# One plain gate pair per layer instead of two in a fp32 decoder trunk, and the block sums of h taken in another order

## The chip, the cores and the metric

The kernel runs on one core of one Trainium2 chip. The metric is the device time in microseconds of one execution, and smaller is better. The core has a matrix engine (TensorE, PE in the profile), a vector engine (VectorE, DVE), a scalar engine (ScalarE, ACT), a general engine (GpSimd, POOL), and queues of DMA transfers that here are issued by SyncE (SP). Each engine has its own list of instructions and takes them in the order of that list; semaphores tie the lists together.

## The reference

Two layers of a decoder trunk over 1024 tokens with 1024 features, all in fp32:

```
h = rmsnorm(x, norm1[l])
proj = h @ w_in[l]                      # q, k, v of two mixers, and gate_pre (2 x 1024 columns)
o_a = dilated_mixture(...)              # 12 heads: near and far windows, ALiBi softmax
o_b = stick_breaking_attention(...)     # 4 heads: sigmoid(z) times a running product of 1 - sigmoid(z)
gates = sigmoid(gate_pre + b_gate[l])
merged = g_a * (o_a @ w_br[l, :256]) + g_b * (o_b @ w_br[l, 256:])
x = x + merged @ w_o[l]
h2 = rmsnorm(x, norm2[l])               # then a gated FFN with a causal conv, and its residual
```

After the layers comes a last rmsnorm. What matters here is the product `h @ w_in[l]`, above all its 2048 gate columns, and the stick-breaking attention that runs beside it.

## The kernel before, in words

**Precision.** Every fp32 operand of a product is split in two: `split` (L136 to L149) casts the high part on ACT (L139) and subtracts it on DVE to get the low part (L146). A product then takes three matmuls per block of 128 rows: high by high, high by low, low by high.

**Plain and seven.** The feature-major h of one layer stands in SBUF as `hh`, `hl` for two token halves n = 0, 1 (tags hh0, hl0, hh1, hl1), each with 8 blocks of 128 features. `gate(l, c)` (L1207) computes one block of 128 gate columns plainly: two halves of 8 blocks by three matmuls, 48 matmuls of 512 columns. `pair(...)` (L1053) computes two such blocks together by Strassen's scheme in the form with seven products (`seven`, L980): seven products of 4 blocks by three matmuls, 84 matmuls of 512 columns where two plain blocks take 96. For that it needs sums of the quarters of the weights (made on POOL at L1075, L1076 and on DVE at L1080, L1085, and split by `piece`) and sums of the quarters of h.

**The sums of h** are made once per layer by `block_sums` (L989). The quarters are b11, b12, b21, b22 (b11 is half 1, first four blocks; b12 half 0, first four; b21 half 1, last four; b22 half 0, last four). The program's S[1] is b12 - b11, S[2] is b22 - S[1], S[3] is b22 - b12, and S[4] is b21 - S[2]. `first(t, a, b, i)` makes block i of S[1] or S[3] on POOL with three additions (L999, L1004, L1005), `second(i)` makes S[2] on DVE from S[1] in place (L1012, L1013), `fourth(i)` makes S[4] on DVE (L1019 to L1021) into the room of a quarter of h that is no longer needed. `in_two(t, i)` splits a block. In the kernel before, POOL makes the four blocks of S[3] and then the four of S[1]; the splits of S[3] come when the head is over, and S[1] and S[2] follow at a set pace.

**The order of a mixer.** `mixer` (L1229) first drives the head (`head`, L593: the values and the first key and query columns, all plain). Then `attend` walks the attention items: 16 stick items, 4 near items, 16 far items. Between the matmuls of the attention it puts steps of the class `Dense`, at a rate for each kind of item (`RATE`, `RATE_N`, `RATE_T`). `Dense.choose` takes the plain gates first, then the pairs of `main`, and when those are through the gate pairs of `seven`. `PLAIN` is the number of plain blocks (two for each gate pair), and `EARLY` how many of the gate pairs stand early in `main` instead of in the last list. `Dense.side` is the list of the work on the sums; one entry is taken at each step for which its condition holds, and what is left when the first pair starts is done at once. The last dense steps, `finish`, run after the attention.

**Who decides the order.** PE's order is the order of the program. The other engines' lists are put in order by the planner of the framework, by priorities and its own estimate of times.

**Rooms that matter.** The tag `s` has two PSUM banks, for the scores z of the attention: a z can only be written when ACT has read the z two before it, as `beta` (L687) and as `stay` (L688). The tag `xa` has four rooms in SBUF: `kv`, `slots`, a `stay` tile for each stick item, and the sum for S[3]. The tag `ql` has two: the values `vb` of the head, the sum for S[1] and S[2], and the weights `in_a` of each pair. The first column block of each score is masked by POOL (L691); DVE then runs the product along each row (the scan at L704) and multiplies (L708); PE turns the result (`sb_t`, L716) and applies it to the values (`sb_o`, L729).

Of the kernel before, what the change touches and what calls it, by code (L numbers as in the profile page):

```python
# [42 lines left out]
SECOND = 0.35  # L43
RATE = (1.1, 1.25, 1.35, 1.4)
RATE_N = 0.75
RATE_T = 0.6
PLAIN = 4
EARLY = 3
LEAD = 6
LEAD_N = 7  # L50
LEAD_T = 3
# [6 lines left out]
def f32(ap):  # L58
    return ap.bitcast(F32)
# [3 lines left out]
def trunk_kernel(ctx, tc, x, norm1, w_in, b_gate, w_br, w_o, norm2, w_up, conv_w, conv_b, w_down, norm_f, out, depth=None, probe=None):  # L63
# [59 lines left out]
    def bank(tag, name):  # L123
        return ps.tile([P, 512], F32, tag=tag, name=name)
# [4 lines left out]
    def big(name, dtype=F32):  # L129
        return sb.tile([P, 2, T], dtype, tag="e8", bufs=6, name=name)  # L130

    def quarter(name, dtype=F32, c=HF):
        return sb.tile([P, 2048 // c, c], dtype, tag="xa", bufs=4, name=name)
# [41 lines left out]
    def product(o, pairs, first=True, last=True, share=False):  # L175

        n = len(pairs)
        quantum = 2 * 512 // o.shape[-1]
        for i, ((lh, ll), (rh, rl)) in enumerate(pairs):
            pe.matmul(o, lh, rh, start=(first and i == 0), stop=False, skip_group_check=share)  # L180
            pe.matmul(o, lh, rl, start=False, stop=False, skip_group_check=share)  # L181
            pe.matmul(o, ll, rh, start=False, stop=(last and i == n - 1), skip_group_check=share)  # L182
            if i % quantum == quantum - 1 and i < n - 1:
                yield
# [249 lines left out]
    def h_part(n, k):  # L434
        return H[n][0][:, k, :], H[n][1][:, k, :]
# [105 lines left out]
    R = {}  # L541

    def new_v(name):
        return [sb.tile([P, 4, 4, P], F32R, tag="ql", bufs=2, name=name) for _ in range(2)]

    def values_part(vt, w, ms):
        for m in ms:
            o = bank("ps", "v_ps")
            for j in range(2):
                t = 2 * m + j  # L550
                n, c = t // 4, t % 4
                tok = slice(c * P, (c + 1) * P)
                pairs = []
                for k in range(KD):
                    hh, hl = h_part(n, k)
                    pairs.append(((hh[:, tok], hl[:, tok]), w[k]))
                yield from product(o[:, j * 256 : (j + 1) * 256], pairs)
                if j == 0:
                    yield
            ov = o.rearrange("p (j h c) -> p h j c", j=2, h=4)  # L560
            vv = vt[m // 2][:, :, 2 * (m % 2) : 2 * (m % 2) + 2, :]
            one = act.copy(vv[:, :, :, 0:64], ov)
            two = dve.tensor_tensor(vv[:, :, :, 64:128], ov, f32(vv[:, :, :, 0:64]), ALU.subtract)
            LAST["head"] = one.ins.name, two.ins.name
            if m % 2:
                nc.sync.dma_start(sv[0][:, :, 2 * m - 2 : 2 * m + 2, :], f32(vt[m // 2]))
            yield
# [25 lines left out]
    def head(l):  # L593


        def place(n, name):
            x = [big(name, F32R) for _ in range(n)]
            return ([x[0][:, h, :] for h in range(2)] if n == 1 else [y.rearrange("p a b -> p (a b)") for y in x])

        wv = weights(w_in[l][:, OFF_VB : OFF_VB + 256], 256, place(2, "v_w")) if l else early.pop("wv")  # L600
        others = lambda: [weights(w_in[l][:, off : off + P], P, place(1, "kq_w"), None if l else pool) for off in (OFF_KB, OFF_QB)]
        if l:
            wk, wq = others()
        yield
        vt = new_v("vb")
        if l:
            yield from values_part(vt, wv, range(2))
        else:
            yield from values_part(vt, wv, range(1))
            wk, wq = others()  # L610
            yield from values_part(vt, wv, range(1, 2))
        for n in range(2):
            yield from kq_half(0, wk, n)
            yield from kq_half(1, wq, n)
            if n == 0 and not l:
                yield from values_part(vt, wv, range(2, 4))
        if l:
            yield from values_part(vt, wv, range(2, 4))

    def scores(o, qt, ql, k):  # L620
# [368 lines left out]
    def block_sums(dense):  # L989


        last, rs = {}, {}

        def first(t, a, b, i):
            if i == 0:
                new_s(t)
                rs[t] = quarter("h_sum") if t == 3 else sb.tile([P, 4, HF], F32, tag="ql", bufs=2, name="h_sum")
            r, (ah, al), (bh, bl) = rs[t][:, i, :], a()[i], b()[i]
            one = pool.tensor_tensor(r, f32(al), f32(bl), ALU.subtract)  # L999
            if last:  # L1000
                tc.add_manual_dep(one.ins, last["sum"], NO_SYNC, reason="one sum after the other")
            else:
                tc.add_manual_dep(one.ins, LAST["h"], SYNC, reason="after h")
            pool.tensor_tensor(r, r, f32(ah), ALU.add)  # L1004
            last["sum"] = pool.tensor_tensor(r, r, f32(bh), ALU.subtract).ins.name  # L1005

        def second(i):
            if i == 0:
                new_s(2)
            in_two(1, i)  # L1010
            r, (ah, al) = rs[1][:, i, :], b22()[i]
            dve.tensor_tensor(r, f32(ah), r, ALU.subtract)  # L1012
            dve.tensor_tensor(r, r, f32(al), ALU.add)  # L1013

        def fourth(i):
            if i == 0:
                S[4] = half(0, 0)
            r, (ah, al) = small("h_sum"), b21()[i]
            dve.tensor_tensor(r, f32(ah), f32(S[2][i][0]), ALU.subtract)  # L1019
            dve.tensor_tensor(r, r, f32(S[2][i][1]), ALU.subtract)  # L1020
            dve.tensor_tensor(r, r, f32(al), ALU.add)  # L1021
            split(*S[4][i], r, "waits")

        def in_two(t, i):
            split(*S[t][i], rs[3 if t == 3 else 1][:, i, :], "waits", LAST["head"])

        b11, b12, b21, b22 = (lambda n=n, k=k: half(n, k) for k in range(2) for n in (1, 0))
        todo = []

        def series(after, lag, gap, f, g):  # L1030

            at = {}
            for i in range(4):
                at.setdefault(i * gap, []).append(lambda i=i: f(i))
                at.setdefault(i * gap + lag, []).append(lambda i=i: g(i))
            for k in range(3 * gap + lag + 1):
                todo.append((after, lambda fs=at.get(k, ()): [h() for h in fs]))

        for i in range(4):
            todo.append((set(), lambda i=i: first(3, b22, b12, i)))  # L1040
        for i in range(4):
            todo.append(({"head"}, lambda i=i: in_two(3, i)))
        series({"head"}, 5, 2, lambda i: first(1, b12, b11, i), second)
        for i in range(4):
            todo.append((set(), lambda i=i: in_two(2, i)))

        def begin():
            for i in range(4):
                dense.at(1 + 2 * i, lambda i=i: fourth(i))

        return todo, begin

    def pair(dense, l, offs, tiled, put):  # L1053

# [174 lines left out]
    def mixer(l, pending):  # L1229
        R.clear()  # L1230
        vectors = setup(l)
        dense = Dense()
        dense.plain = [gate(l, c) for c in range(PLAIN)]
        gates = [pair_gate(dense, l, e) for e in range(PLAIN // 2, KD)]
        dense.seven = gates[EARLY:]
        dense.side, dense.begin = block_sums(dense)
        dense.done |= {"K0", "K1", "V0", "V1", "V2", "V3"}
        if l:
            next(vectors)
# [24 lines left out]
        for _ in vectors:  # L1264
            pass
        dense.main = [
            *((None, set(), f, True) for f in (pair_near(dense, l, 2), *gates[:EARLY], pair_v(dense, l, 0), pair_near(dense, l, 4), pair_near(dense, l, 6))),
            *((None, set(), f, True) for f in (pair_v(dense, l, 1), pair_kq(dense, l, 1, 0), pair_kq(dense, l, 2, 0))),
# [7 lines left out]
        for pr in range(2):  # L1276
            share = {}
            for i in range(8):
                if i % 4 == 0:
                    share = {}  # L1280
                items.append((f"T{pr}{i}", [f"F{8 * pr + i}"], [], RATE_T, lambda pr=pr, i=i, share=share: far_item(dense, pr, i // 4, i % 4, share)))
        dense.fetch()
# [8 lines left out]
        def in_two(nm, halves=range(2)):  # L1291
            src = R["ob" if nm == "b" else "on"]
            if nm not in oh:
                oh[nm] = big("oh_" + nm, F32R), big("ol_" + nm, F32R)
            hi, lo = oh[nm]
            for n in halves:
                for c in range(2):
                    sl = slice(n * HF, (n + 1) * HF)
                    one = split(hi[:, c, sl], lo[:, c, sl], src[:, c, sl])
                    if nm == "b" and n:  # L1300
                        yields(one)

        branches()
        todo = [(n, e0 + i) for e0 in range(0, KD, 2) for n in range(2) for i in range(2)]
# [782 lines left out]
```

## Time and profile before

| | |
|---|---|
| Median of 3 runs | 2643.44 us (2640.93 to 2643.49) |
| The profiled execution, its own time | 2642.11 us |
| Its span, first to last instruction | 2640.1 us |
| Granted TensorE clock, mean | 1.000 |
| Layer 0: end of the head, first plain gate matmul | 65.0 us |
| Layer 0: first matmul of a pair | 120.5 us |
| Layer 1: first plain gate matmul | 1370.9 us |
| Layer 1: first matmul of a pair | 1424.9 us |

How to read the rows: a timeline row has the start in us from the start of the span, the duration in us, the engine, the line, the operation, the tiles written and read, the shape, and in brackets the idle time before it and what ended it. Matmuls overlap in the pipeline, so what one costs is read from the distance between starts and not from its own duration. A row of the waits has who waited for whom, the total in us, the number of times, and the longest.

### The profile page before, as it was taken

How to read it: one execution, taken by the hardware profiler on the slowest of the kernel's cores; microseconds unless marked ns; L12 is line 12 of the kernel's file. 1: busy time of each engine (PE TensorE's matmuls, PEld its weight loads, DVE VectorE, ACT ScalarE, POOL GpSimd, SP SyncE). 2: the span in 40 equal slices, each digit the busy share in tenths (PEclk: the TensorE clock that was granted, in tenths of full speed). 3: DMA queues.
4: the chain of work that ended last, by engine and by line, in shares of the span. 5: the costliest groups of instructions: out<-in, count | busy, mean ns of one | idle time of the engine just before them, and what ended most of it. 6: DMA issues, size and time to landing. Idle time of an engine off the chain costs nothing.

```text
span 2640.1 us, 36792 instructions
## 1 busy us (share of the span) xinstructions
PE 2621.5 (99%) x12780; PEld 2192.0 (83%) x12780; DVE 2068.6 (78%) x3094; ACT 1337.7 (51%) x2488; POOL 734.9 (28%) x612
## 2 busy tenths in 40 slices
PE   9999999999999999999999999999999999999999
PEld 8888888888888888888888888888888888888888
DVE  5887766795888898897659787667858888888865
ACT  5555565564545555432435555666645455554225
POOL 5422201132244343321162212101321343334200
PEclk9999999999999999999999999999999999999999
DMA  7343587873244444688442445797632544357863
GB/s 259 114 144 112 159 220 204 220 253 90 81 146 146 164 146 157 234 310 322 155 154 93 145 140 160 198 236 203 219 101 80 168 144 159 136 176 256 330 247 116
DMA packets 400550, 468.25 MB, mean 177 GB/s; under 512 B 24437, under 2 KB 315629, under 8 KB 398573
## 3 DMA queue, kind: packets, MB, share of 16 engines
q1 hardware_dynamic: 400348, 465.90, 54.9%
q8 instruction: 101, 1.65, 0.3%
q14 instruction: 85, 0.69, 0.1%
q10 hardware_dynamic: 16, 0.00, 0.0%
HBM read 303.23 MB, written 162.59 MB: 176 GB/s over the span
## 4 chain that ended last, share of the span: by engine, by line
PE 83%; DVE 9%; issue 3%; DMA 2%; ACT 2%; POOL 1%; SPq 0%; DVEq 0%; POOLq 0%; ACTq 0%
PE u_a L983 5%; PE u_a L985 5%; PE u_a L984 5%; PE d_ps L1715 5%; PE d_ps L1716 5%; PE d_ps L1717 5%; PE i_a L983 4%; PE i_a L985 4%; PE i_a L984 4%; PE u_c L985 3%; PE u_c L983 3%; PE u_c L984 3%; PE o_ps L180 2%; PE o_ps L181 2%; PE o_ps L182 2%
## 5 line engine op out<-in xcount | busy, mean ns | idle before, releaser
L146 DVE TENSOR_TENSOR w_lo<-up_a,w_hi 128x512 fp32r<-128x512 f32 x240 | 236.7, 992 | 20.2 <-ACT w_hi L139 20.2
L139 ACT CAST w_hi<-up_a 128x512 fp32r<-128x512 f32 x240 | 149.4, 623 | 183.9 <-PE u_a L984 45.9
L1723 DVE TENSOR_TENSOR x<-x,d_ps 128x512 f32<-128x512 f32 (+1 forms) x228 | 151.8, 671 | 78.0 <-PE d_ps L1717 76.6
L1454 POOL TENSOR_TENSOR cv<-cv 128x512 f32<-128x512 f32 x88 | 131.8, 1509 | 248.8 <-DVE cv L1449 138.9
L139 ACT CAST w_hi<-in_a 128x512 fp32r<-128x512 f32 x192 | 119.2, 621 | 117.5 <-PE i_c L984 42.7
L146 DVE TENSOR_TENSOR w_lo<-in_a,w_hi 128x512 fp32r<-128x512 f32 x192 | 141.3, 736 | 36.4 <-ACT w_hi L139 27.0
L146 DVE TENSOR_TENSOR g<-cv,g 128x512 fp32r<-128x512 f32 x154 | 151.7, 986 | 5.2 <-ACT g L139 2.8
L1715 PE MATMUL d_ps<-gd_in,w_hi 128*128 128x512 f32 (+1 forms) x340 | 130.3, 383 | 2.3 <-ACT w_hi L139 1.4
L1717 PE MATMUL d_ps<-gd_in,w_lo 128*128 128x512 f32 (+1 forms) x340 | 129.8, 382 | 0.0
L1716 PE MATMUL d_ps<-gd_in,w_hi 128*128 128x512 f32 (+1 forms) x340 | 129.8, 382 | 0.0
L1075 POOL TENSOR_TENSOR u<-in_a 128x512 f32<-128x512 f32 x32 | 45.8, 1431 | 293.2 <-DMA in_a<-in_w_in_dram 110.5
L983 PE MATMUL u_a<-hh,w_hi 128*128 128x512 f32 x320 | 124.7, 390 | 0.4 <-DVE u L1605 0.3
L984 PE MATMUL u_a<-t_lo,w_hi 128*128 128x512 f32 x320 | 124.5, 389 | 0.0
L985 PE MATMUL u_a<-t_hi,w_lo 128*128 128x512 f32 x320 | 124.5, 389 | 0.0
L985 PE MATMUL u_a<-hh,w_lo 128*128 128x512 f32 x320 | 124.5, 389 | 0.0
L983 PE MATMUL u_a<-t_hi,w_hi 128*128 128x512 f32 x320 | 124.5, 389 | 0.0
L984 PE MATMUL u_a<-hl,w_hi 128*128 128x512 f32 x320 | 124.5, 389 | 0.0
L146 DVE TENSOR_TENSOR w_lo<-w_raw,w_hi 128x512 fp32r<-128x512 f32 x96 | 77.5, 809 | 57.6 <-ACT w_hi L139 52.8
L691 POOL TENSOR_SCALAR_AFFINE_SELECT beta<-beta 128x128 f32<-128x128 f32 x64 | 36.6, 571 | 305.2 <-ACT beta L687 305.2
L139 ACT CAST g<-cv 128x512 fp32r<-128x512 f32 x154 | 94.9, 616 | 39.8 <-POOL cv L1454 29.3
L1715 PE MATMUL d_ps<-gd_in,wd 128*128 128x512 f32 (+1 forms) x292 | 113.9, 390 | 0.0
L1717 PE MATMUL d_ps<-gd_in,wd 128*128 128x512 f32 (+1 forms) x292 | 112.8, 386 | 0.0
(395 smaller groups left out, 8638.0 us busy)
## 6 DMA issues: line engine op xcount, KB each, us to landing
gd<-g SPq DMA_DIRECT2D x154, 512.0 KB, 3.1
gd_in<-gd SPq DMA_DIRECT2D x154, 512.0 KB, 6.3
up_a<-in_w_up_dram SPq DMA_DIRECT2D x80, 512.0 KB, 5.6
in_a<-in_w_in_dram SPq DMA_DIRECT2D x64, 512.0 KB, 5.4
wd_raw<-in_w_down_dram SPq DMA_DIRECT2D x22, 1024.0 KB
gin<-gs SPq DMA_DIRECT2D x32, 512.0 KB, 5.1
w_raw<-in_w_o_dram SPq DMA_DIRECT2D x64, 256.0 KB, 2.9
t_kq<-tk SPq DMA_DIRECT2D x32, 384.0 KB, 5.0
```

The lines of the kernel that those rows point to most:

```text
L139: one = act.copy(hi, src)
L146: two = dve.tensor_tensor(lo, src, f32(hi), ALU.subtract)
L180: pe.matmul(o, lh, rh, start=(first and i == 0), stop=False, skip_group_check=share)
L181: pe.matmul(o, lh, rl, start=False, stop=False, skip_group_check=share)
L983: pe.matmul(o, w[0][:, c], rh, start=(first and i == 0), stop=False, skip_group_check=True)
L984: pe.matmul(o, w[0][:, c], rl, start=False, stop=False, skip_group_check=True)
L985: pe.matmul(o, w[1][:, c], rh, start=False, stop=(last and i == 3), skip_group_check=True)
L1454: return lambda: pool.tensor_tensor(dst, a, b, ALU.subtract)
L1715: pe.matmul(o[:, sub], wh[:, c], gh[:, sub], start=(i == 0 and k in (0, 4, 5)), stop=False, skip_group_check=True)
L1716: pe.matmul(o[:, sub], wh[:, c], gl[:, sub], start=False, stop=False, skip_group_check=True)
L1717: pe.matmul(o[:, sub], wl[:, c], gh[:, sub], start=False, stop=(i == m - 1), skip_group_check=True)
L1723: dve.tensor_tensor(x, x, o[:, sub], ALU.add)
```

## The change

Four constants change, `RATE_T` from 0.6 to 0.55, `PLAIN` from 4 to 2, `EARLY` from 3 to 4. Per layer, one gate pair that was two plain blocks becomes a pair by seven products, and of the seven gate pairs four stand in `main` (three of six before). The order of the work on the sums changes: POOL makes S[1] first, in a new function `mid` that the head calls, together with the splits of S[1]'s first two blocks. The third split, and S[3] on POOL, follow when the head is over (`go`), then S[2] with the last split of S[1] and the splits of S[2] (`later`), and the splits of S[3] last. In layer 0 `mid` is called behind the last values of the head, with the second half of the keys and queries still to come; in layer 1 it is called ahead of the last values.

```
-RATE_T = 0.6
-PLAIN = 4
-EARLY = 3
+RATE_T = 0.55
+PLAIN = 2
+EARLY = 4
 ...
             yield from kq_half(1, wq, n)
             if n == 0 and not l:
                 yield from values_part(vt, wv, range(2, 4))
+                R["mid"]()
         if l:
+            R["mid"]()
             yield from values_part(vt, wv, range(2, 4))
 ...
         def second(i):
             if i == 0:
                 new_s(2)
-            in_two(1, i)
             r, (ah, al) = rs[1][:, i, :], b22()[i]
 ...
-        todo = []
-        def series(after, lag, gap, f, g):
-            at = {}
-            for i in range(4):
-                at.setdefault(i * gap, []).append(lambda i=i: f(i))
-                at.setdefault(i * gap + lag, []).append(lambda i=i: g(i))
-            for k in range(3 * gap + lag + 1):
-                todo.append((after, lambda fs=at.get(k, ()): [h() for h in fs]))
-        for i in range(4):
-            todo.append((set(), lambda i=i: first(3, b22, b12, i)))
-        for i in range(4):
-            todo.append(({"head"}, lambda i=i: in_two(3, i)))
-        series({"head"}, 5, 2, lambda i: first(1, b12, b11, i), second)
-        for i in range(4):
-            todo.append((set(), lambda i=i: in_two(2, i)))
+        def mid():
+            for i in range(4):
+                first(1, b12, b11, i)
+            for i in range(2):
+                in_two(1, i)
+        def go():
+            in_two(1, 2)
+            for i in range(4):
+                first(3, b22, b12, i)
+        def later(i):
+            second(i)
+            if i == 0:
+                in_two(1, 3)
+            else:
+                in_two(2, i - 1)
+        todo = [({"head"}, go)]
+        todo += [(set(), lambda i=i: later(i)) for i in range(4)]
+        todo += [(set(), lambda: in_two(2, 3))]
+        todo += [(set(), lambda i=i: in_two(3, i)) for i in range(4)]
 ...
-        return todo, begin
+        return todo, begin, mid
 ...
-        dense.side, dense.begin = block_sums(dense)
+        dense.side, dense.begin, R["mid"] = block_sums(dense)
```

## The prediction

> **What bounds the kernel now.** I read the totals of the page first, then TensorE's own waits.
>
> ```profile
> PE 2621.5 (99%) x12780; PEld 2192.0 (83%) x12780; DVE 2068.6 (78%) x3094; ACT 1337.7 (51%) x2488; POOL 734.9 (28%) x612
> ```
>
> ```profile
> PE z L621 <- ACT stay L688: 2.7, 5, 1.1
> ...
> PE u_ps L181 <- DVE hl L536: 1.3, 2, 0.7
> ...
> PE o L900 <- DVE p1l L146: 0.4, 2, 0.2
> ```
>
> PE is busy 2621.5 of 2640.1 us, and the longest group of its waits is 2.7 us in all. So a matmul less is time less, and a wait that PE gains is never given back: nothing behind it has slack on PE to take it in. I work against the profiled execution (2642.11 us by its own time, 2 us of it outside the span); the median of the runs shown is 1.3 us above, and the difference that I find is put on the median.
>
> **The gain.** One key product of 24 matmuls of 512 columns runs between these two starts:
>
> ```profile
> 1342.31 0.39 PE L180 MATMUL q_ps<-hh,kq_w 128*128 128x512 f32 x1
> ...
> 1347.75 0.39 PE L180 MATMUL kq_ps<-hh,kq_w 128*128 128x512 f32 x1
> ```
>
> 5.44 us for 24 is 0.227 us each. A plain pair takes 96, a pair by seven 84, so a layer loses 12 and the kernel 24, **-5.4 us** (the built lists of PE differ by just these 24). 0.2% of this kernel, about what a measurement can tell from no change, is 5.3 us, so the gain alone would stand on the edge of it. Transfers for the weights stay at 1 MB a pair. A pair by seven adds to DVE 7 splits, 2 sums and 3 additions, and saves 4 splits; to ACT 7 casts and 4 copies for 4 casts and 4 copies; to POOL 2 sums. With DVE at 78% and PE hardly waiting for it, I put these at nothing where they are spread out; what they cost without cover is a rival below. The lower `RATE_T` and the later place of one gate pair move dense work from the far items into the end of the attention: the same matmuls, between -1 and +1 us, as PE's wait there now is 0.4 us in all (o, L900), taken as 0.
>
> **The first wait: layer 0.** What changes is what stands ahead of the first scores. In the built lists of the changed kernel, ACT has this order in layer 0 (tiles' numbers left out; in brackets whom it waits for):
>
> ```
> t_hi<-h_sum x3  (blocks 0 to 2 of S[3]) [Pool]
> t_hi<-h_sum, gt<-g_ps, t_hi<-h_sum
> w_hi<-in_a      (first weight piece)
> w_hi<-in_a      (the summed piece)      [Pool]
> gt<-g_ps, table load, beta<-z, stay<-z
> ```
>
> The second `w_hi` casts what POOL writes at L1076, and POOL's list has the eight sums, then L1075 and L1076 of the first pair. Both were far from the first scores before, because there 192 plain matmuls stood ahead of the first pair; now it is 96. The first scores need not wait for the pair, but they stand behind it on ACT.
>
> ```profile
> 43.26 1.30 POOL L999 TENSOR_TENSOR h_sum<-hl 128x512 f32<-128x512 f32 x1 [14.11 <-DVE hl L146]
> 44.61 0.95 POOL L648 MEMSET slots<- 64x1024 f32 x1
> 45.64 1.29 POOL L1004 TENSOR_TENSOR h_sum<-h_sum,hh 128x512 f32<-128x512 f32 x1
> ...
> 75.17 1.74 POOL L999 TENSOR_TENSOR h_sum<-hl,hl 128x512 f32<-128x512 f32 x1
> ...
> 78.68 1.27 POOL L1005 TENSOR_TENSOR h_sum<-h_sum,hh 128x512 f32<-128x512 f32 x1
> ...
> 98.46 1.30 POOL L1075 TENSOR_TENSOR u<-in_a 128x512 f32<-128x512 f32 x1 [4.73 <-DVE w_lo L146]
> 99.84 1.63 POOL L1076 TENSOR_TENSOR in_a<-in_a 128x512 f32<-128x512 f32 x1
> ```
>
> ```profile
> 76.03 0.62 ACT L139 CAST w_hi<-w_raw 128x512 fp32r<-128x512 f32 x1 [2.10 <-PE g_ps L181]
> 76.56 0.58 ACT L1216 COPY gt<-g_ps 128x512 f32<-128x512 f32 x1
> 77.15 1.28 ACT L687 ACT_TABLE_LOAD   x1
> 78.45 0.60 ACT L687 ACTIVATE beta<-z 128x512 f32<-128x512 f32 x1
> 78.94 0.59 ACT L688 ACTIVATE stay<-z 128x512 f32<-128x512 f32 x1
> ```
>
> The sums run from 43.26 to 79.95. The memset inside them (1.03 us to the next start) now stands ahead of them, in the 14.11 us in which POOL was idle: they end near 78.9. L1075 and L1076 take 101.47 - 98.46 = 3.0: 81.9. The cast then starts near 82.0, and `gt` 0.53 later, as 76.03 and 76.56 show: 82.55. From the start of `gt` to the third z on PE, which needs the bank that `stay` reads, it is
>
> ```profile
> 79.58 0.50 PE L621 MATMUL z<-kv,slots 128*128 128x512 f32 x1 [1.07 <-ACT stay L688]
> ```
>
> 79.58 - 76.56 = 3.02: so z starts near 85.6 and not at 79.58, **+6.0 us**. From both sides: the slowest block of sums above takes 79.95 - 75.17 = 4.78 us; in layer 1 one starts at 1362.49 and the next at 1366.49, 4.0 us.
>
> ```profile
> 1362.49 1.30 POOL L999 TENSOR_TENSOR h_sum<-hl,hl 128x512 f32<-128x512 f32 x1
> ...
> 1366.49 1.29 POOL L999 TENSOR_TENSOR h_sum<-hl,hl 128x512 f32<-128x512 f32 x1
> ```
>
> Eight at 4.0 end at 75.3 (+2.4), eight at 4.78 at 81.5 (+8.6). I keep 6.0, since the mix of this very stretch gave it. POOL's list has one more thing ahead of the first masks, L1075 of the second pair, whose weights can only be fetched when the last block of S[2] is split, near 79:
>
> ```profile
> in_a<-in_w_in_dram SPq DMA_DIRECT2D x64, 512.0 KB, 5.4
> ```
>
> They land near 84.4, ahead of the first `beta` and `stay` (85.0 and 85.5 by the row of ACT above), so I cost that at nothing; landing later, it would hold back the scans and `sb_t` by as much as it is late beyond some 2 us. In layer 1 ACT's list has the first betas ahead of both casts, and POOL's has the first masks ahead of the pair's sums, so no such wait is there; the second mask stands behind the pair's sums there, so its scan comes later by part of their 3.0 us, which eats the slack ahead of `sb_t` (taken as 0, at most those 3.0 us).
>
> **What the gap does to the clock.** PE would stand idle from 78.5 to 85.6, 7 us. The trace has one such gap, at its end:
>
> ```profile
> 2634.00:2636.00 2.00, 0.67 (x7) 0.43 (x4) 1.57 (x3) 1.30 (x3) 0.00 (x0) 1.00 0.59 224
> 2636.00:2641.00 5.00, 0.00 (x0) 0.00 (x0) 0.00 (x0) 0.00 (x0) 0.00 (x0) 0.69 0.52 196
> ```
>
> The columns are PE, PEld, DVE, ACT and POOL busy, the granted clock, and DMA. PE ends at 2634.67, and the clock falls in the 5 us that follow: 0.31 of 5 us is 1.55 us of full speed lost. If the clock falls in the gap of layer 0 too, PE starts slowly behind it. I take **+1.5 us**, between 0 (it falls and recovers within the gap) and 3 (the loss of that row twice).
>
> The Trainium skill (TensorE: Matmul & The Clock Gate, Part 1: The HAM clock gate) says that an idle window of about 3.4 us halves the clock, and that a busy window of that length must pass until it is full again. The fall at the end of this trace agrees with the first half; no row here shows the second. By it the price is half of 3.4 to 6.8 us, an estimate of 1.7 to 3.4 us, and the sum would be up to 1.9 us above mine.
>
> **The second wait: both layers.** Its rows, from the timelines of PE and of DVE in both layers:
>
> ```profile
> 85.72 0.49 PE L716 MATMUL sb_t<-ident,beta 128*128 128x128 f32 x3
> ...
> 89.26 0.40 PE L621 MATMUL z<-kv,slots 128*128 128x512 f32 x1
> ...
> 1390.11 0.49 PE L716 MATMUL sb_t<-ident,beta 128*128 128x128 f32 x3
> ...
> 1393.66 0.40 PE L621 MATMUL z<-kv,slots 128*128 128x512 f32 x1
> ```
>
> ```profile
> 66.21 6.50 DVE L146 TENSOR_TENSOR t_lo<-h_sum,t_hi 128x512 fp32r<-128x512 f32 x4
> ...
> 90.54 0.68 DVE L708 TENSOR_TENSOR beta<-beta,stay 128x511 f32<-128x511 f32 x1
> 91.14 0.68 DVE L146 TENSOR_TENSOR t_lo<-h_sum,t_hi 128x512 fp32r<-128x512 f32 x1
> ...
> 124.84 1.77 DVE L146 TENSOR_TENSOR w_lo<-u,w_hi 128x512 fp32r<-128x512 f32 x1
> ...
> 1395.54 0.68 DVE L146 TENSOR_TENSOR t_lo<-h_sum,t_hi 128x512 fp32r<-128x512 f32 x1
> ```
>
> The second stick item's `stay` takes the room of S[3]'s sum. Before, that sum was split at 66.21 to 72.71, long ahead. Now its fourth block is split late: ACT's list has `t_hi` of the block, `sbh`, `w_hi` (the third weight piece), and only then `stay<-z` [DVE, ACT, Pool] of the second item's first row; DVE's has `sbl`, two scans, `beta`, `sbl`, `beta`, `w_lo`, and then `t_lo` of the block. PE's next z needs the bank that this `stay` reads.
>
> From `sb_t` to z PE has 89.26 - 85.72 = 3.54 us of other work. DVE reaches the place of `w_lo` at 91.14, 5.42 behind `sb_t`; `w_lo` takes 0.60 to the next start, `t_lo` 0.68: 6.70. `stay` 0.59 more and 0.05 to PE: 7.35. PE waits 7.35 - 3.54 = 3.8 us. Layer 1 has the same distances (`sb_t` 1390.11, z 1393.66, DVE's place 1395.54), so **+7.6 us** for both. Bounds: were DVE free, the cast of `w_hi`, which waits for the plain matmuls just ahead of z, still puts 0.62 + 0.60 + 0.68 + 0.59 + 0.05 = 2.5 us behind it; `w_lo` and `t_lo` in their slow form (1.77 for 0.68, row 124.84) give 6.0. Queued behind the waiting `stay` on ACT are the next betas and `gt`, all late by the same 3.8 us and needed later still.
>
> **Sum:** -5.4 + 6.0 + 1.5 + 7.6 = +9.7 us: 2651.8 against the profiled execution, **2653** against the median. Slower by 0.37%.
>
> **The rivals.** The last of them rests on this row, busy times and clock from 65 to 160 us:
>
> ```profile
> 65.00:160.00 95.00, 93.11 (x451) 76.02 (x451) 84.45 (x120) 54.19 (x110) 37.59 (x38) 1.00 0.40 125
> ```
>
> - *Only the first wait comes* (the scheduler's wait of `stay` is met early, because `t_lo` is through before the scans): -5.4 + 7.5 = +2.1, 2645.5. For it: the block's sum is ready before 80; against it: DVE's list. Chance 0.10.
> - *Only the second comes* (POOL is through with the pair's sums by 79, or the stall on z is short): -5.4 + 7.6 = +2.2, 2645.6. POOL would have to end its sums at 75.9, near the fast bound. Chance 0.10.
> - *Faster: the waits are for earlier events than I read.* The lists name the engine that is waited for, not which of its instructions. If ACT's cast and `stay` wait for POOL's and DVE's work of a block before, both waits end ahead of PE's need, at 78.5 and 89.3; then only the 24 matmuls count: 2638.0. It decides at the point where DVE's `t_lo` and POOL's L1076 end ahead of those times. Against it: both are read-after-write or a room that is reused, and they need the last one. Chance 0.08.
> - *DVE becomes the bound* in the first pairs: 8 more instructions a layer at 0.68 are 5.4 us on an engine that is busy 84.45 of 95 us there; uncovered in both layers this adds 10.9: 2664. PE's longest group of waits for DVE is 1.3 us in the whole span, so it is not near. Chance 0.06.
>
> That the change does not do what it says is excluded by the 24 matmuls.
>
> **How the numbers follow.** Forecast, both waits: 0.66, its own range 2645 (-5.4 + 2.4 + 0 + 5.0) to 2662 (its upper bounds together, 18.2, are unlikely at once, so I stop at 2660). The two rivals at 2645.5 belong inside, 2 us to each side for the terms that I took as 0: 2643.5 to 2660 leaves out less than 2 in 10. Faster by over 0.2% (below 2638.2): the third rival, most of its 0.08, so 0.07. Within 0.2%: the first two, and the low end of the forecast, 0.21. Slower by over 0.2% (above 2648.7): 0.72.
>
> **What would show it.** In the changed kernel's timeline of layer 0 the third z starts near 85 to 86 with an idle of about 7 us and ACT's `stay` as its end; behind it matmuls start more than 0.227 us apart for some us. In both layers the z behind `sb_t` waits some 3.8 us for ACT's `stay`. PE's waits for that group rise from 2.7 to about 16 us. The forecast is wrong if POOL's L1076 ends by 78, if DVE's `t_lo` of S[3]'s last block ends ahead of z, or if later stages lose PE's waits that they have now.

## The result and the profile after

The changed kernel takes 2679.70 us (median of 4 runs, 2678.94 to 2682.52) against 2642.86 us for the kernel before, run beside it (4 runs, 2640.93 to 2643.49): a ratio of 1.0143, 95% interval 1.0125 to 1.0160. It is slower by 36.8 us. I had forecast the sign and a quarter of the size: slower by 9.7 us, in a range that ended at 2660.

The profiled execution, the slowest of the four, took 2682.52 us by its own time, with a span of 2680.8 us (2640.1 before). The first row is the page's totals, the others are PE's own waits over the whole span (total in us, times, longest):

```profile
PE 2629.8 (98%) x12756; PEld 2194.3 (82%) x12756; DVE 2095.6 (78%) x3110; ACT 1345.2 (50%) x2494; POOL 744.4 (28%) x616
```

```profile
PE z L623 <- ACT stay L690: 13.4, 8, 5.6
PE sb_t L718 <- DVE beta L710: 6.5, 5, 1.7
PE v_t L1176 <- DVE vv L1182: 4.1, 4, 1.2
PE g_ps L180 <- DVE kq_l L582: 3.6, 1, 3.6
PE z L623 <- DMA t_kq<-tk: 3.6, 4, 1.9
PE o L902 <- ACT p1h L139: 2.9, 2, 1.4
```

The 24 matmuls are gone (12756 for 12780), and yet PE is busy 8.3 us longer: for some stretches PE runs at half the clock, which costs 9.5 us by the reckoning below; the other 4 us or so stay open. PE's waits for `stay` rise from 2.7 to 13.4 us, where I had expected about 16, but five more groups stand behind it: four that were not among the kernel before's waits of 0.2 us or more, and the turns of the values (`v_t`), which rise from 0.7 to 4.1 us. (Lines of the changed kernel are some 2 to 5 higher: its `stay` is L690, its weight sums L1080 and L1081.)

Where the time comes from is read from the same matmul in both timelines of PE. Four stretches: from the start to the first `sb_o` of layer 0 (92.69 us before, 109.53 after), from there to the first `br_ps` (550.02, 572.48), from the first `v_ps` of layer 1 (1324.02, 1345.50) to its first `sb_o` (1397.09, 1431.14), and on to its first `br_ps` (1853.72, 1894.52). Each stretch has the same matmuls in all kernels but for the gain, which lies in the two stretches that end at `br_ps`. Each against the kernel before, in us, for all kernels of this study; a row is one execution, and executions of one kernel differ by 2 to 9 us, so small differences between rows mean little:

```
                              layer 0             layer 1
                        to sb_o  to br_ps   to sb_o  to br_ps     span
the change                +16.8     +5.6      +12.6     +6.8     +40.7
e1  order only            +12.4     -1.1       +9.3     -2.0     +17.8
e2  constants only         +7.2    +15.5       +2.2    +16.3     +39.4
e3  RATE_T 0.6            +18.1     -0.3      +12.6      0.0     +31.1
e4  masks first           +13.5     +2.1       +9.3     +3.2     +26.3
e5  splits early          +17.1     +2.9      +11.2     +5.9     +35.9
e7  three repairs         +12.2     -1.4       +7.5     +1.7     +20.3
e6  e7, S[3] on DVE        +7.3     +0.3       +3.0     +1.6     +12.6
e8  before, RATE_T 0.55    +0.1     +1.0        0.0     +0.9      +0.2
e9  e6 with PLAIN 4        +7.3     +1.8       +1.4     +1.0     +12.3
e10 e6 with EARLY 3        +7.4     +9.0       +3.3     +8.0     +28.7
e11 e6, values not held    +4.8     +0.4       +1.8     +0.6      +7.5
```

The start of the attention costs 29.4 us in both layers together, where I had 15.1. The stretches behind it cost 12.4, and since they hold the gain of 5.4, what was lost in them is 17.8, where I had nothing.

**The start of layer 0.** PE's timeline:

```profile
68.76 0.80 PE L180 MATMUL g_ps<-hh,w_hi 128*128 128x512 f32 x1 [3.57 <-DVE kq_l L582]
...
89.33 0.80 PE L623 MATMUL z<-kv,slots 128*128 128x512 f32 x1 [5.65 <-ACT stay L690]
...
97.54 0.30 PE L718 MATMUL sb_t<-ident,beta 128*128 128x128 f32 x1 [0.74 <-POOL beta L693]
99.47 0.69 PE L718 MATMUL sb_t<-ident,beta 128*128 128x128 f32 x2 [1.63 <-DVE beta L710]
...
100.38 0.63 PE L181 MATMUL g_ps<-hl,w_hi 128*128 128x512 f32 x1
100.81 0.63 PE L182 MATMUL g_ps<-hh,w_lo 128*128 128x512 f32 x1
...
105.97 0.50 PE L623 MATMUL z<-kv,slots 128*128 128x512 f32 x1 [1.32 <-ACT stay L690]
```

PE stops five times in 40 us, and between the stops there are stretches in which matmuls start 0.43 us apart (100.38 and 100.81) and not 0.227. The first stop I had not seen at all: PE's first gate matmul needs the bank that `kq_l` reads, and DVE comes to `kq_l` late. DVE's timeline, then POOL's:

```profile
59.59 1.77 DVE L1013 TENSOR_TENSOR h_sum<-hh,h_sum 128x512 f32<-128x512 f32 x1
61.29 1.77 DVE L146 TENSOR_TENSOR w_lo<-w_raw,w_hi 128x512 fp32r<-128x512 f32 x1
62.99 1.77 DVE L1014 TENSOR_TENSOR h_sum<-h_sum,hl 128x512 f32<-128x512 f32 x1
...
66.47 1.64 DVE L1014 TENSOR_TENSOR h_sum<-h_sum,hl 128x512 f32<-128x512 f32 x1
68.03 0.68 DVE L582 TENSOR_TENSOR kq_l<-kq_ps,kq_h 128x512 fp32r<-128x512 f32 x1
...
82.94 1.76 DVE L1014 TENSOR_TENSOR h_sum<-h_sum,hl 128x512 f32<-128x512 f32 x1
```

```profile
62.59 1.62 POOL L1006 TENSOR_TENSOR h_sum<-h_sum,hh 128x512 f32<-128x512 f32 x1
64.29 1.59 POOL L1007 TENSOR_TENSOR h_sum<-h_sum,hh 128x512 f32<-128x512 f32 x1
...
79.15 1.62 POOL L1007 TENSOR_TENSOR h_sum<-h_sum,hh 128x512 f32<-128x512 f32 x1
...
82.55 1.60 POOL L1081 TENSOR_TENSOR in_a<-in_a 128x512 f32<-128x512 f32 x1
92.39 1.29 POOL L1080 TENSOR_TENSOR u<-in_a 128x512 f32<-128x512 f32 x1 [8.24 <-DMA in_a<-in_w_in_dram]
93.64 0.28 POOL L693 TENSOR_SCALAR_AFFINE_SELECT beta<-beta 128x128 f32<-128x128 f32 x1
```

In the new order DVE makes S[2]'s sums while POOL makes S[3]'s, and each of these instructions of DVE takes 1.6 to 1.8 us where it takes 0.68 alone, each of POOL 1.6 to 1.7 where it takes 1.29 alone. So two blocks of S[2]'s sum, four additions, stand in front of `kq_l` and hold it until 68.03; before, it started at 59.74.

The second stop is the wait that I had forecast, with another engine at its end. ACT's timeline:

```profile
84.74 0.62 ACT L139 CAST t_hi<-h_sum 128x512 fp32r<-128x512 f32 x1 [3.98 <-DVE h_sum L1014]
85.26 1.13 ACT L139 CAST w_hi<-in_a 128x512 fp32r<-128x512 f32 x2
86.30 0.58 ACT L1221 COPY gt<-g_ps 128x512 f32<-128x512 f32 x1
...
88.69 0.59 ACT L690 ACTIVATE stay<-z 128x512 f32<-128x512 f32 x1
```

ACT stood ahead of both `w_hi` for the sum of S[2] that DVE ended at 84.70. POOL's L1081 ended at 84.15, so both chains end within 0.6 us of each other, POOL's 2.2 us later than my 81.9. From `gt` (86.30) to z (89.33) it is 3.03 us, as I had it (3.02). The third and fourth stop come from POOL: the second pair's sum stands ahead of the first masks and waits for its weights until 92.39; then come the masks, the scans, the betas, and only then `sb_t`. Those weights were sent for at 86.54, right behind the split of S[2]'s last block, which DVE's slow sums had made late too:

```profile
86.54 1.02 SPq L1072 DMA_DIRECT2D in_a<-in_w_in_dram  x2
```

**Layer 1**, where I had forecast no first wait. PE's timeline, then ACT's:

```profile
1407.92 0.50 PE L623 MATMUL z<-kv,slots 128*128 128x512 f32 x1 [1.16 <-ACT stay L690]
...
1411.79 0.50 PE L623 MATMUL z<-kv,slots 128*128 128x512 f32 x1 [1.00 <-ACT stay L690]
...
1417.80 0.44 PE L718 MATMUL sb_t<-ident,beta 128*128 128x128 f32 x2 [1.70 <-DVE beta L710]
...
1425.02 0.79 PE L623 MATMUL z<-kv,slots 128*128 128x512 f32 x1 [3.56 <-ACT stay L690]
```

```profile
1403.97 0.62 ACT L139 CAST t_hi<-h_sum 128x512 fp32r<-128x512 f32 x1 [5.03 <-DVE h_sum L1014]
...
1410.14 0.62 ACT L139 CAST w_hi<-in_a 128x512 fp32r<-128x512 f32 x1 [1.51 <-DMA in_a<-in_w_in_dram]
...
1424.37 0.77 ACT L690 ACTIVATE stay<-z 128x512 f32<-128x512 f32 x2 [2.49 <-DVE beta L710]
```

The casts of the weights do stand behind the first betas there, as I read; but a `t_hi` of S[2] stands ahead of them, and it waits 5.03 us for DVE's slow sums. The casts also stand ahead of the next betas: the stop of 1.00 us ahead of 1411.79 comes behind the `w_hi` of 1410.14, which waited for its weights.

**The clock.** Half-microsecond windows of the changed kernel, layer 0 (PE, PEld, DVE, ACT, POOL busy, the granted clock, DMA):

```profile
68.50:69.00 0.50, 0.24 (x1) 0.24 (x2) 0.50 (x5) 0.50 (x2) 0.50 (x1) 0.68 0.00 0
72.00:72.50 0.50, 0.50 (x4) 0.41 (x3) 0.50 (x1) 0.00 (x0) 0.42 (x2) 0.91 0.26 87
85.50:86.00 0.50, 0.00 (x0) 0.00 (x0) 0.50 (x2) 0.50 (x2) 0.00 (x0) 0.75 0.00 0
92.50:93.00 0.50, 0.50 (x4) 0.41 (x3) 0.00 (x0) 0.15 (x1) 0.50 (x1) 0.93 0.56 133
99.00:99.50 0.50, 0.03 (x1) 0.03 (x1) 0.41 (x1) 0.00 (x0) 0.00 (x0) 0.90 0.08 25
102.50:103.00 0.50, 0.50 (x5) 0.48 (x4) 0.50 (x1) 0.00 (x0) 0.00 (x0) 0.69 0.00 0
```

These are the windows in which the clock changes between 1.00 and 0.50. If it is 0.50 for a share of the window and 1.00 for the rest, it falls at 68.68, 85.75 and 99.40 and is full again at 72.09, 92.57 and 102.81. PE works in 68.76 to 72.09, 89.33 to 92.57 and 99.47 to 102.81, 9.9 us at half speed: 5.0 us lost, where I had 1.5. With the idle times of the five stops (12.9 us) and without the 1.07 us that the kernel before waits there, this is the whole of the +16.8.

### The profile page after: what moved, and what is told of

Same layout as the page of the kernel before. It is cut to its first block, busy times and chain, and to the rows that moved or that the text cites. A ratio compares the mean times of both kernels' runs of the same rounds, so it can differ in the third digit from the quotient of the medians.

```text
span 2680.8 us, 36744 instructions
## 1 busy us (share of the span) xinstructions
PE 2629.8 (98%) x12756; PEld 2194.3 (82%) x12756; DVE 2095.6 (78%) x3110; ACT 1345.2 (50%) x2494; POOL 744.4 (28%) x616
## 4 chain that ended last, share of the span: by engine, by line
PE 75%; DVE 8%; DMA 4%; issue 3%; ACT 2%; POOL 1%; SPq 0%; DVEq 0%; ACTq 0%; POOLq 0%
PE u_a L985 5%; PE u_a L987 5%; PE u_a L986 5%; PE d_ps L1720 4%; PE d_ps L1721 4%; PE d_ps L1722 4%; PE i_a L985 3%; PE i_a L987 3%; PE i_a L986 3%; PE u_c L987 3%; PE u_c L986 3%; PE u_c L985 3%; PE o_ps L180 2%; PE o_ps L182 2%; PE o_ps L181 2%
## 5 line engine op out<-in xcount | busy, mean ns | idle before, releaser
L139 ACT CAST w_hi<-in_a 128x512 fp32r<-128x512 f32 x204 | 126.5, 620 | 140.3 <-PE i_c L986 43.2
L146 DVE TENSOR_TENSOR w_lo<-in_a,w_hi 128x512 fp32r<-128x512 f32 x204 | 147.4, 723 | 33.6 <-ACT w_hi L139 30.3
L1080 POOL TENSOR_TENSOR u<-in_a 128x512 f32<-128x512 f32 x34 | 46.8, 1377 | 336.9 <-DMA in_a<-in_w_in_dram 148.3
L706 DVE TENSOR_TENSOR_SCAN stay<-stay,zero 128x512 f32<-128x512 f32 (+2 forms) x96 | 101.5, 1065 | 41.7 <-POOL stay L693 41.7
L985 PE MATMUL i_a<-hh,w_hi 128*128 128x512 f32 x272 | 112.8, 415 | 0.0
```

Source lines behind the costliest of these rows:

```text
L139: one = act.copy(hi, src)
L146: two = dve.tensor_tensor(lo, src, f32(hi), ALU.subtract)
L706: one = dve.tensor_tensor_scan(rev, rev, zero[:, 0:1].to_broadcast([P, c1 - c0]), 1.0 if c1 == L else sv[:, c1 : c1 + 1], ALU.mult, ALU.add)
L985: pe.matmul(o, w[0][:, c], rh, start=(first and i == 0), stop=False, skip_group_check=True)
```

## The experiments

The theory after the result, **A**: the sums and splits of h need their time, and 96 matmuls per layer fewer stand between them and the first scores; what is late follows from that. The rivals, **B**: the new order costs by itself, since it lets DVE and POOL slow each other; **C**: the lower rate of the far items makes the waits in the later stretches.

### e1 and e2: the two halves of the change alone

e1 is the changed kernel with the old constants:

```
-RATE_T = 0.55
-PLAIN = 2
-EARLY = 4
+RATE_T = 0.6
+PLAIN = 4
+EARLY = 3
```

> The new order of the sums alone, with the old constants (PLAIN 4, EARLY 3, RATE_T 0.6). Theory A (the loss comes from the 96 matmuls that no longer stand between the sums and the first scores): close to the kernel before, 2640 to 2647 us. Theory B (the new order itself costs, since it lets DVE's and POOL's sums run at the same time and slow each other): most of the 37 us stay, over 2655 us.

Measured: 2660.56 us, ratio 1.0066 (1.0051 to 1.0081). e2 is the kernel before with the three new constants.

> The changed constants alone (PLAIN 2, EARLY 4, RATE_T 0.55), with the old order of the sums. Theory A: the waits at the first scores are there as in the changed kernel or worse, since the old order ends later: 2670 to 2695 us. Theory B: the gain of 24 matmuls is seen, 2635 to 2645 us.

Measured: 2680.50 us, ratio 1.0142 (1.0127 to 1.0157). PE's waits, first of e1, then of e2:

```profile
PE z L623 <- ACT stay L690: 9.3, 4, 2.6
PE g_ps L180 <- DVE kq_l L582: 4.6, 1, 4.6
```

```profile
PE z L621 <- ACT stay L688: 7.1, 3, 6.6
PE i_c L984 <- DVE t_lo L146: 6.0, 4, 1.6
PE i_c L983 <- ACT u L1098: 4.3, 2, 2.5
```

Neither theory is right alone. The order by itself costs 17 us, all of it at the start of the two layers, and with the full 192 plain matmuls in place: this is what B said, and nearly half of the loss in size. That the slowing of DVE and POOL is its reason, e1 alone does not show. The constants by themselves cost as much as the whole change, 36.8 us, so A holds too. The two do not add up: in the old order the first pair stands on the matmuls of S[2] (`i_c` waits for `t_lo`) and most of the loss lies behind the first `sb_o` (+15.5 and +16.3); in the new order S[2] is ready for the pair and most of the loss lies ahead of it (+16.8 and +12.6). So the new order moved most of the wait from the pairs to the scores. Most, since in layer 0 of e2 PE stops once at the scores as well, for 6.64 us ahead of the third z at 85.38. That is close to the wait that I had forecast, which I had priced with the durations of the old order.

### e3 and e8: the rate of the far items

e3 is the changed kernel with `RATE_T` back at 0.6, e8 the kernel before with `RATE_T` at 0.55.

> The changed kernel with RATE_T back at 0.6. PE's idle time in the stages behind the stick items is about 14 us more than before over both layers. Theory C (the lower rate takes the dense work away from the far items and so opens these waits): 2665 to 2672 us. Theory A (the waits come from the start of the attention and from the place of the pairs): 2677 to 2682 us, no change that can be told.

> The kernel before with RATE_T 0.55 alone. My step put the lower rate at -1 to +1 us: 2641 to 2646 us. If the rate costs by itself what it costs in the changed kernel (9.7 us): 2651 to 2655 us.

Measured: e3 2670.00 us, 9.7 below the change; ratio to the kernel before 1.0100 (1.0083 to 1.0117). e8 2641.96 us, ratio 0.9996 (0.9987 to 1.0006), no difference. So C holds in the changed kernel and not in the kernel before. PE's waits over the far items of layer 1, in the changed kernel (1745 to 1900 us) and then in e3 (1735 to 1890 us):

```profile
PE z L623 <- DMA t_kq<-tk: 2.2, 2, 1.9
PE o L902 <- ACT p1h L139: 1.4, 1, 1.4
```

```profile
PE o L902 <- DVE p1l L146: 0.2, 1, 0.2
```

With less dense work between the steps of a far item, PE comes to the next score before its transfer has landed, and to `o` before ACT has cast `p1h`; at the higher rate both waits are gone there. In layer 0 the changed kernel has 1.4 us of each, e3 0.3 us of the first and none of the second. The clock adds to it: behind the longest of these stops, 1.91 us ahead of 1808.79, it is at half from 1809.48 to 1812.89, by the same reckoning as above, and PE works all that time: 1.7 us more. Why the kernel before stands the lower rate is not shown.

### e4 and e5: the masks, and the second wait

e4 puts a pair's two sums on POOL behind the masks that are issued before them:

```
+                            LAST["mask"] = one.ins.name
...
-        pool.tensor_tensor(u2, a11, a21, ALU.subtract)
+        one = pool.tensor_tensor(u2, a11, a21, ALU.subtract)
+        if "mask" in LAST:
+            tc.add_manual_dep(one.ins, LAST["mask"], NO_SYNC, reason="behind the masks")
```

> The changed kernel, with a pair's two sums on POOL placed behind the masks that were issued before. My step that cost the second pair's sum ahead of the first masks at nothing would then hold: 2678 to 2682 us. If the wait of that sum for its weights holds the masks, the scans and sb_t (first mask at 93.64 us in layer 0 though its beta was there at 88.8): 4 to 5 us less in layer 0 and 2 to 3 us less in layer 1, with the clock: 2668 to 2674 us.

Measured: 2670.17 us, 9.5 below the change (ratio to before 1.0102, 1.0087 to 1.0117). POOL's first mask comes at 86.50 and not at 93.64:

```profile
86.50 0.29 POOL L693 TENSOR_SCALAR_AFFINE_SELECT beta<-beta 128x128 f32<-128x128 f32 x1 [5.39 <-ACT beta L689]
```

The table shows 3.3 us less in each of the two starts and 3.5 in each of the two stretches behind them (13.8 in all, more than the 9.5 of the medians, since e4's profiled execution is one of its faster ones and the change's its slowest). The edit moves the first pair's sums as well: in layer 0 POOL now makes them at 87.24, behind the first masks, the cast of the summed piece comes behind the first betas, and the stop ahead of the third z falls from 5.65 to 1.93 us. So the 9.5 us are the price of the first pair's sums and of the later ones together, and no run parts them. That the sums of later pairs had been holding masks too is a reading of the stretches behind the start, and not shown.

e5 issues all splits before the first scores:

```
         dense.done.add("head")
+        while dense.side:
+            dense.aside()
```

> The changed kernel, with all splits of the sums issued before the first scores, so that the second item's stay need not wait for the split of the last block of S[3]'s sum. If my second wait is what PE waits for there, the idles of 1.32 us (104.25 us, layer 0) and 3.56 us (1421.07 us, layer 1) go, with one or two drops of the clock of 1.7 us: 2672 to 2676 us. If the later splits were only the last of several things that stay waits for: 2678 to 2682 us.

Measured: 2679.21 us, ratio 1.0132 (1.0117 to 1.0147): no gain. The wait of z for the second item's `stay` is gone, as it should be, and PE waits elsewhere:

```profile
PE sb_t L718 <- DVE beta L710: 12.8, 7, 4.5
PE z L623 <- ACT stay L690: 5.4, 6, 2.3
```

In e4, where `sb_t` is not late, the second wait stands alone: PE waits 2.60 us for the `stay` of the second item at 101.00, and ACT's `stay` begins when the first item's last `beta` is through on DVE. One more instruction of DVE, `w_lo`, stands between that `beta` and the `t_lo` that I had named. The room of S[3]'s sum was still taken, as I said, since `t_lo` read it at 100.75, later than this `stay` began (100.35); so, by elimination, `stay` got the room of the first item's `stay`, which that `beta` reads.

### e7 and e6: repairs together, and S[3]'s sum on DVE

e7 has `RATE_T` 0.6, e4's and e5's edits together. e6 is e7 with S[3]'s sum made by DVE:

```
-            one = pool.tensor_tensor(r, f32(al), f32(bl), ALU.subtract)
-            if last:
+            eng = pool if t == 1 else dve
+            one = eng.tensor_tensor(r, f32(al), f32(bl), ALU.subtract)
+            if t == 3:
+                pass
+            elif last:
...
-            pool.tensor_tensor(r, r, f32(ah), ALU.add)
-            last["sum"] = pool.tensor_tensor(r, r, f32(bh), ALU.subtract).ins.name
+            eng.tensor_tensor(r, r, f32(ah), ALU.add)
+            last["sum"] = eng.tensor_tensor(r, r, f32(bh), ALU.subtract).ins.name
```

> The changed kernel with three repairs together: RATE_T 0.6, a pair's two sums behind the masks, all splits before the first scores. The first two measured alone took off 9.7 and 9.5 us. If they are separate: 2652 to 2660 us. If they cure the same waits: 2662 to 2670 us.

> As the next run, and S[3]'s sum made by DVE beside POOL's S[1], so that POOL is through with its sums some 20 us earlier and DVE's sums of S[2] no longer run beside POOL's. If the two engines' slow forms (1.77 for 0.68 us on DVE, 1.6 to 1.75 for 1.29 us on POOL) make the waits at the start (kq_l 3.57 us, first z 5.65 us, with the clock), these go too: 2632 to 2644 us. If the length of the chain of sums and splits makes them, whoever does it: no better than the next run, 2652 to 2662 us.

Measured: e7 2662.59 us, ratio 1.0071 (1.0056 to 1.0086); e6 2654.65 us, ratio 1.0041 (1.0026 to 1.0056). By the numbers e7 lies in the second band, at its lower edge. Yet the three take off 17.1 us where the rate and the masks alone gave 9.7 and 9.5, so these two are separate but for 2 us; that the early splits bring nothing on top is likely from e5, but no run has the two without them. S[3] on DVE takes off another 7.9 us, and e6 too lies in the second band, which stood for the length of the chain. DVE's, POOL's and PE's rows of e6:

```profile
65.97 1.28 DVE L1017 TENSOR_TENSOR h_sum<-hh,h_sum 128x512 f32<-128x512 f32 x2
```

```profile
62.06 1.63 POOL L1011 TENSOR_TENSOR h_sum<-h_sum,hh 128x512 f32<-128x512 f32 x1
```

```profile
PE kq_ps L180 <- DVE vb L563: 4.2, 1, 4.2
```

POOL is through at 63.69 and not at 80.77 as in the changed kernel, and from there DVE makes two additions of S[2]'s sum in 1.28 us. The wait for `kq_l` is gone from PE's list, and that for `stay` is 0.5 us in all. So the same work, placed so that DVE and POOL overlap less long, takes the start of layer 1 from +7.5 to +3.0 us. The edit does two things at once, though: the overlap is shorter, and POOL has only half of the sums to make, so it does not show how much of the 7.9 us the slowing alone is worth. It is not free: while POOL makes S[1], S[3]'s sums on DVE are slow too, and they now hold the eviction `vb` in the head, for which PE waits 4.2 us. And it does not reach the time before, which the first band stood for: 11.9 us are left.

### e9, e10 and e11: what is left

e9 is e6 with PLAIN 4 and EARLY 3, e10 is e6 with EARLY 3 alone, e11 is e6 with the last two blocks of S[3]'s sum on DVE behind the evictions `vb`:

```
+            LAST["vb", m] = two.ins.name
...
             if t == 3:
-                pass
+                if i > 1:
+                    tc.add_manual_dep(one.ins, LAST["vb", i], NO_SYNC, reason="behind vb")
```

> The repaired kernel (RATE_T 0.6, masks ahead of the pairs' sums, splits early, S[3]'s sum on DVE; 2654.7 us) with PLAIN 4 and EARLY 3 again. Theory A (what is left of the loss comes from the pairs by seven that start 96 matmuls earlier, beside the first items): near the kernel before but for the wait in the head of 4.2 us, 2643 to 2649 us. Theory B (it comes from the new order even as repaired): the 24 matmuls come back on top, 2656 to 2662 us.

> The repaired kernel (2654.7 us) with EARLY 3 for 4, one pair of gates later. If the fourth gate pair ahead of the values' pair makes the small waits between 100 and 600 us (about 3 us a layer): 2648 to 2652 us. If its place does not matter: 2653 to 2657 us.

> The repaired kernel (2654.7 us) with the last two blocks of S[3]'s sum on DVE placed behind the evictions vb, for which PE's kq_ps waited 4.2 us in the head of layer 0. If that wait is the whole effect: 2649 to 2652 us. If the later blocks then end too late for the first scores and the wait moves there: 2653 to 2657 us. In neither case faster than the kernel before.

Measured: e9 2653.73 us, ratio 1.0043 (1.0028 to 1.0058); e10 2669.20 us, ratio 1.0099 (1.0084 to 1.0114); e11 2650.93 us, ratio 1.0034 (1.0020 to 1.0048).

e9 lies between its two bands and cannot be told from e6. So with the sums out of the way the constants, with their 24 matmuls less, are worth nothing that can be told: something takes back what the matmuls save. The table puts it in layer 1 up to `sb_o` (+3.0 in e6, +1.4 in e9) and in the stretches behind (with the gain of 2.7 us in each, e6's +0.3 and +1.6 are 3.0 and 4.3 us lost, where e9 has 1.8 and 1.0). That it is the pairs, which start earlier beside the stick items, is my reading; no run shows it alone. And since e9 has all the constants of the kernel before, its 11.1 us are the price of the new order even as repaired. e10 goes the other way than I expected, 14.6 us slower than e6; PE's waits of e10:

```profile
PE v_t L1182 <- DVE vv L1188: 14.8, 10, 4.9
```

With one gate pair fewer ahead of it the values' pair comes earlier (in layer 0 its first `v_t` is at 223.1 and not at 246.8), and its turns wait for DVE's `vv`. The raised `EARLY` belongs to the lower `PLAIN`. In e11 the wait of 4.2 us for `vb` is gone, but one of 1.7 us for `kq_l` is back. Its median is 3.7 us below e6's, in the first band; the intervals of the two overlap. It is the fastest of the versions with fewer matmuls and still 8.3 us behind the kernel before: nothing here points to one that beats both.

## Why the prediction was wrong

Both waits that I had forecast came, so the sign was no luck. The step that failed is the price of the start of the attention: I worked out when the sums would be ready from instructions as they ran in the old order and from POOL's chain alone, while in the new order DVE's sums and POOL's slow each other, and I put what follows at nothing. The start cost 29.4 us in both layers where I had 15.1. The stretches behind it lost 17.8 us where I had none. By terms:

- **The gain, -5.4 us.** The 24 matmuls are gone, at the size that I gave them, but even in the repaired kernel their time is not won: e6 against e9 shows no difference.
- **The first wait in layer 0, +6.0.** Its place, its end on PE and the 3.02 us from `gt` to z were right. What ended it was mis-read: I took POOL's chain with the mix of durations from before. DVE's list had the sums of S[2] beside it, in their slow form. My sum did not price them; the slow form stands only in my upper bound of the second wait. With the stop at `kq_l`, for which my sum had no term, PE is idle 9.2 us up to the third z and not 7.1.
- **Layer 1 has no first wait: wrong.** I looked only for the casts of the weights ahead of the betas; the `t_hi` of S[2] was there too, behind DVE. With the late `sb_t` PE's stops there, ahead of the second wait, are 4.5 us (0.40, 1.16, 1.00, 0.24 and 1.70).
- **The clock, +1.5.** I counted one gap. In layer 0 the clock was at half three times while PE worked: 5.0 us. In layer 1 it was at half from 1423.8 to 1430.6 by the same reckoning, and PE worked from 1425.02: 2.8 us. With the 1.7 us of the far items it is 9.5 us in all. The six edges above lie on a grid: they are 3.41, 13.66, 6.82, 6.83 and 3.41 us apart, all multiples of 3.41. The Trainium skill (TensorE: Matmul & The Clock Gate, Part 1: The HAM clock gate) says that the clock is set by a free-running window of 4096 cycles, about 3.4 us; the edges agree with it. What I missed is that short stops add up: in the 3.41 us up to 85.75 and in those up to 99.40 PE was busy for 1.35 and 1.11 us, and the clock fell all the same.
- **The second wait, +7.6.** It came, with 1.32 us in layer 0 and 3.56 in layer 1, and 2.60 where it stands alone (e4). `stay` waited for the first item's last `beta` and not for `t_lo`, so two instructions of DVE, `w_lo` and `t_lo`, fall out of my sum of 3.8. e5 shows that it is not worth its length: without it PE waits longer for `sb_t` (12.8 us in all, 6.5 in the change).
- **Costed at nothing, the second pair's sum ahead of the masks.** I had S[2]'s last split near 79 and so the weights land at 84.4; they were sent for at 86.54, and the sum began at 92.39. That is 8 us late, and I had said what this would do: hold back the scans and `sb_t`. Moving the pairs' sums, the first pair's among them, behind the masks is worth 9.5 us (e4).
- **Costed at nothing, the lower rate, -1 to +1.** True of the kernel before (e8), not of the changed one: 9.7 us (e3). Of what I put at nothing and one run prices, this and the masks are the largest.
- **The rival in which DVE becomes the bound** came nearest in kind and in size: DVE's instructions ahead of the scores are what is late. But it counted the 8 instructions that the new pairs add, and the late ones are the sums of S[2], which are no more than before and take 1.77 us each.

What stays open: how much of the loss at the start the slowing of DVE and POOL makes by itself, why the lower rate hurts in the changed kernel and not in the kernel before, and which of the many waits of 0.2 to 1.5 us in e11 make up the rest of its 8.3 us.

## What to carry to other kernels

When work on one engine is moved so that it runs beside another engine's, look in the trace for that instruction's duration beside the other engine at work and without it, and price the chain with the one that it will have. Where a change shortens the stretch that covers a chain of preparation, count how long the chain is and not what stands last in it; another order of the same chain only moves the wait to whoever needs its last piece. And an edit that costs nothing in the kernel as it is can cost in the kernel as changed: price it there, or make it in a step of its own.

## What the runs showed of the hardware

DVE and POOL take turns. While both run additions or subtractions of two tiles in SBUF, an instruction of DVE starts every 1.70 us (59.59, 61.29 and 62.99 in the changed kernel) and one of POOL as well (62.59 above, 64.29 next): one for one, where DVE alone starts one every 0.60 us (86.43, 87.03 and 87.64). But `kq_l`, which reads one of its two inputs from PSUM, takes its 0.68 us at 68.03 beside a POOL at work. The Trainium skill (SBUF — State Buffer, SBUF: two separate sides) says that a DVE instruction with two inputs in SBUF and a POOL instruction that reads SBUF lock a shared pair of ports against each other, "an exclusive lock, not a bandwidth split"; these rows agree with it in kind. But an instruction of each, one behind the other, would make 1.9 us and not 1.70, by the 0.60 and about 1.33 us from start to start where each runs alone (POOL, seven starts from 42.96 to 50.95). The rule would have told me that the new order of the sums slows both engines.

The clock of PE changed only on a grid of 3.413 us in the changed kernel: from the edge at 102.81 to that at 1809.48 it is 500 such steps. What a stop cost beyond itself hung on the step that it fell in. The stop of 3.57 us ahead of 68.76 covers a whole step (65.27 to 68.68) and cost 1.7 us more than itself; the one of 1.32 us ahead of 105.97 cost nothing more, and in its step (102.81 to 106.22) PE was busy for 2.09 us. Of all steps of this kernel at the full clock, those with PE busy for 1.40 us or less (0.00, 1.35, 1.11, 1.10, 1.40) were followed by half the clock, and those with 1.85 us or more were not. The border is not that sharp in the other runs: a step with 1.90 us was followed by half the clock in e7, one with 1.61 us was not in e5.
